# Weight loads traced as far as raw tiles are free, an eighth raw tile, and 128-row bias products in the expert stage

## The chip, the cores and the metric

One core of one Trainium2 chip runs the whole program in one launch. The metric is the device time of that launch in microseconds (us); the time before is the median of three runs. The engines are TensorE (PE, its weight loads are PEld), VectorE (DVE), ScalarE (ACT), GpSimd (POOL) and SyncE (SP, which issues nearly all DMAs).

## What is computed

The reference is a chain of two blocks over 512 tokens of width 1024, all in float32. The part that the change touches is the mixture of experts at the end of the first block:

```python
logits = h @ w_router + b_router              # 512 tokens, 32 experts
top_val, top_idx = lax.top_k(logits, 4)
gates = softmax(top_val)
# for each expert e, on the rows xb that chose it:
u   = xb @ w1[e] + b1[e]                       # 1024 -> 2048
glu = minimum(u[:, 0::2], 7.0); lin = clip(u[:, 1::2], -7.0, 7.0)
act = glu * sigmoid(1.702 * glu) * (lin + 1.0)
y   = act @ w2[e] + b2[e]                      # 1024 -> 1024
# out[token] += gate * y
```

Before it stand a token mixer (recurrence, Fourier mixing) with its output projection; behind it two layers of attention (three branches), gates and projections.

## The kernel before, in words

The 32 experts are sorted by how many tokens chose them; a rank has a fixed number of rows (`CAP`, L1246): 192 for ranks 0 to 5, 128 for ranks 6 to 14, 64 for the rest. Ranks run in groups (`sequence`, L1259). Six groups have four ranks A, B, C, D: A has 192 rows, C has 128, B and D have 64. Two groups have three ranks (64, 128, 64 rows) and one has two (64, 128). The order inside a group is written out by hand (`order`, L1276): four column blocks of w1 (0 to 3) and two of w2 (4, 5) for each rank. In most four-rank groups A and B alternate first, then C and D alternate, then the w2 blocks follow.

A block of 512 columns is worked off in four parts of 256 weight rows. Each part is one raw tile of 128 x 2 x 512 floats, 512 KB. `Weights` (L1296) streams them: `load` (L1305) has SP issue the DMA into a tile of the pool `wraw` (seven tiles), `split` (L1316) makes a high and a low half of it (`whi` by ACT on L1324, `wlo` by DVE on L1328 and POOL on L1329) in a pool of four, and `next` (L1352) hands the oldest part to the matmuls. Ranks of 128 rows (`whole`, L1254) take the raw tile itself (L1702), so it is free only when their matmuls are done. Ranks of 64 or 192 rows take the two halves (L1706, L1707, L1709), so the raw tile is free when it is split. `ahead` (L1338) says how far loads and splits are traced ahead of use: before, loads up to seven parts, splits up to three. After that a scheduler orders each engine's instructions; each engine runs its own list in order and waits on semaphores where a tile is not ready or not yet free. SP's list in this stage is the 768 weight loads and a few others.

In `up` (L1822) the first matmul of each accumulation is the bias (L1833): its stationary side is a selection of this rank's row of `b1`, 64 rows (32 of the high half, 32 of the low). For 64-row blocks POOL copies that selection into `mhalf` first (L1827). `consts2` (L1417) loads and splits `b1`; `route` (L1489) makes `perm`. `swiglu` (L1711) runs behind each w1 block: ACT `us`, DVE `gl` and `ln`, ACT `sg`, POOL `ln` (L1728), and then PE transposes `ln` (L1687) for w2. `overflow` (L2007) stands ahead of the expert loop and is a branch that is not taken with these inputs (no instruction inside it is in the trace).

The second block has its own `Weights` with three raw tiles and the same class (L3084).

Of the kernel before, what the change touches and what calls it, by code (L numbers as in the profile page):

```python
# [8 lines left out]
F = mybir.dt.float32  # L9
R = mybir.dt.float32r  # L10
# [1285 lines left out]
class Weights:  # L1296


    def __init__(self, tc, ctx, raw=7, parts=4, kn=2, side="left"):
        self.tc, self.nc, self.kn = tc, tc.nc, kn  # L1300
        self.nraw, self.nsplit = raw, parts - 1
        self.raw = ctx.enter_context(tc.tile_pool(name="wraw", bufs=raw, side=side, reuse_waits="tile"))
        self.par = ctx.enter_context(tc.tile_pool(name="wpar", bufs=parts, side=side, reuse_waits="tile"))
# [31 lines left out]

    reach = 4

    def ahead(self, loads, splits):  # L1338
        while len(self.loads) < min(self.used + loads, len(self.parts)):
            m, k0 = self.parts[len(self.loads)][:2]  # L1340
            self.loads.append(self.load(m(), k0))
        isplit = lambda j: self.parts[j][-1] is not False
        n = sum(isplit(j) for j in range(self.used, len(self.splits)))
        while len(self.splits) < min(len(self.loads), self.used + self.reach):
            j = len(self.splits)
            if isplit(j):
                if n >= splits:
                    break
                n += 1
            self.splits.append(self.split(self.loads[j]) if isplit(j) else self.loads[j][0])  # L1350

    def next(self, splits=None):  # L1352
        self.ahead(self.nraw, self.nsplit if splits is None else splits)
        out = self.splits[self.used]
        self.used += 1
        return out


def consts_moe():
# [10 lines left out]
    lim = np.array([[float(max(128 * j, CAP[r])) if 128 * (j + 1) > CAP[r] else 1e6 for r in range(32) for j in range(4)]], np.float32)  # L1370
    two = np.concatenate([iota[:, :64], iota[:, :64]], 1)
    return {"m_cap": caps, "m_tri": tri, "m_tie": tie, "m_first": first, "m_iota": iota, "m_two": two, "m_tok": tok, "m_lim": lim}


class Moe:
# [13 lines left out]
    def consts(self):  # L1389
# [8 lines left out]
        nc.sync.dma_start(self.iota, rowbc(I["m_iota"], 512))  # L1398
        self.two = c.tile([128, 128], F, name="mtwo")
        nc.sync.dma_start(self.two, rowbc(I["m_two"], 128))  # L1400
        self.tokf = c.tile([128, 5], F, name="mtokf")
# [9 lines left out]
        nc.sync.dma_start(self.br, rowbc(I["b_router"][0:1, :], 32))  # L1411
        self.cap = c.tile([128, 32], F, name="mcap")
        nc.sync.dma_start(self.cap, rowbc(I["m_cap"], 32))
        self.wr = c.tile([128, 8, 32], F, name="mwr")
        nc.sync.dma_start(self.wr, I["w_router"][0].rearrange("(k p) e -> p k e", p=128))

    def consts2(self, pool):  # L1417

        nc, I, c = self.nc, self.i, self.c
        self.halves = [c.tile([64, 128], R, name=f"mhalf{a}") for a in range(2)]  # L1420
        self.b1 = c.tile([64, 2048], R, name="mb1")
        zero = pool.tile([64, 128], F, name="mz", tag="mz", bufs=1)
        nc.gpsimd.memset(zero, 0.0)
        for t in self.halves:
            nc.gpsimd.tensor_copy(t, zero)
        for a in range(2):
            t = pool.tile([128, 1024], F, name="mb1r", tag="fxh", bufs=2)
            s = slice(a * 1024, (a + 1) * 1024)
            t = t[0:32]
            nc.sync.dma_start(t, I["b1"][0][:, s])  # L1430
            nc.scalar.activation(self.b1[0:32, s], t, AF.Copy)
            nc.gpsimd.tensor_tensor(self.b1[32:64, s], t, self.b1[0:32, s].bitcast(F), op=OP.subtract)

# [55 lines left out]
    def route(self):  # L1489
# [37 lines left out]
        nc.vector.tensor_scalar(perm, self.iota[:32, :E], rank, None, op0=OP.is_equal)  # L1527
        self.perm = c.tile([64, E], R, name="permr")
        nc.vector.tensor_copy(self.perm[0:32], perm)
        nc.vector.tensor_copy(self.perm[32:64], perm)  # L1530
        dr = tt.tile([32, E], F, name="drank")
# [100 lines left out]
    def hots(self, r0, n, start, two, posm=None):  # L1632

        nc = self.nc
        iob = (self.two if two else self.iota)[:, None, :128].to_broadcast([128, n, 128])
        hot = []
        for t in range(4):
            h = self.g.tile([128, 4, 128], BF, name="hot", tag="hot", bufs=4)
            src = (self.posm if posm is None else posm)[:, t, r0:r0 + n]
            if start:  # L1640
                s2 = self.g.tile([128, 8], F, name="hots", tag="hots", bufs=4)
                nc.vector.tensor_scalar(s2[:, :n], src, -float(start), None, op0=OP.add)
                src = s2[:, :n]
            nc.vector.tensor_tensor(h[:, :n], iob, src[:, :, None].to_broadcast([128, n, 128]), op=OP.is_equal)
            hot.append(h)
# [65 lines left out]
    def swiglu(self, ps, act, c, tag=None):  # L1711
# [8 lines left out]
        v = ps.rearrange("p (n a) -> p n a", a=2)  # L1720
        gl = x_.tile([128, 256], F, name="gl", tag="gl", bufs=2)
        ln = x_.tile([128, 256], F, name="ln", tag="ln", bufs=3)
        sg = x_.tile([128, 256], F, name="sg", tag="sgm", bufs=2)
        nc.vector.tensor_scalar(gl[:m], v[:, :, 0], 7.0, None, op0=OP.min)  # L1724
# [31 lines left out]
    def plan(self, before):  # L1756
# [23 lines left out]

        first = [(lambda m=m: [m], k0) for m, k0 in before]
        self.W.stream(first + sum([parts(r, a, cc) for g in sequence() for a, r, cc in order(g)], []))

    def experts(self, hD, x1, gt2):
# [37 lines left out]
        def up(r, cc):  # L1822
# [3 lines left out]
            if cc == 0 and not whole(r):  # L1826
                nc.gpsimd.tensor_copy(half[:, 0:64], self.perm[:, r:r + 1].bitcast(F).to_broadcast([64, 64]))  # L1827
            for k0 in range(0, 8, kn):
                w = self.W.next()
                for p, xx in zip(ps, x):  # L1830
                    if k0 == 0:
                        pm = half if xx.n == 64 else self.perm[:, r:r + 1].to_broadcast([64, 128])
                        nc.tensor.matmul(p, pm, self.b1[:, cc * 512:(cc + 1) * 512], start=True, stop=False)  # L1833
                    self.mm_part(p, xx, w, k0, False, k0 + kn == 8)
# [114 lines left out]
        for t in range(4):  # L1949
            for a in range(2):  # L1950
                nc.scalar.activation(self.acc[t][:, a * 512:(a + 1) * 512], self.iota, AF.Copy, scale=0.0)
        self.overflow(hD)
        gs = groups()
        where = {r: min(sum(not whole(q) for q in g[:j]), 1) for g in seq for j, r in enumerate(g)}
# [52 lines left out]
    def overflow(self, hD):  # L2007
# [9 lines left out]
        with tc.If(ne > 0):  # L2017
# [19 lines left out]
            with tc.For_i(0, 128, 1) as i:  # L2037
                te = x_.tile([1, 2], I32, name="te", tag="te", bufs=1)
                nc.sync.dma_start(te, tD[bass.ds(i, 1), :])
                on = nc.values_load(te[0:1, 0:1], min_val=0, max_val=1)  # L2040
                with tc.If(on > 0):
                    e = nc.values_load(te[0:1, 1:2], engines=[ET.SP], min_val=0, max_val=31)
                    ix = x_.tile([128, 1], I32, name="ix", tag="ix", bufs=1)
                    nc.sync.dma_start(ix, iD[bass.ds(i, 1), :].rearrange("a p -> p a"))
# [25 lines left out]
            nc.vector.tensor_tensor(row, self.later[3], offs[:, None, :].to_broadcast([128, 4, 32]), op=OP.add)  # L2070

            over = c.tile([128, 4, 32], F, name="over")
            nc.vector.tensor_tensor(over, self.later[3], self.cap[:, None, :].to_broadcast([128, 4, 32]), op=OP.is_ge)
            gto = self.pick(over, "gto", x_, "y")
# [1034 lines left out]
```

## Time and profile before

| what | value |
|---|---|
| three runs | 3784.77, 3789.82, 3796.57 us (median 3789.82) |
| the profiled execution | 3795.27 us |
| its span, first to last instruction | 3793.5 us, TensorE clock granted 0.924 on average |
| busy share of the span | PE 90%, PEld 66%, DVE 66%, ACT 45%, POOL 46% |
| weight loads of the experts | 768, first issued at 706.0 us, last at 2375.1 us |
| second block, 2500 to 3700 us | PE busy 1176.8 of 1200 us, clock 1.00, DMA share 0.26 |

Matmuls are pipelined, and the profile models their ends: a busy PE is not a PE at its peak. What a matmul costs in a full stream is the distance from its start to the next start. The DMA share is the mean busy share of the core's 16 DMA engines.

### The profile page before, as it was taken

Reading aid. Unit: us, or ns where it says so; the run is one execution under the profiler, and the core shown is the slowest. Engines: PE = TensorE matmul, PEld = TensorE weight load, DVE = VectorE, ACT = ScalarE, POOL = GpSimd, SP = SyncE. Lnnn points to the kernel's source line nnn. Section 1 sums busy time; section 2 is a strip of 40 time slices with the busy share of each in tenths; the row PEclk is TensorE's granted clock in tenths of the full one; section 3 lists DMA queues with packets and bytes.
Section 4 is the critical chain, followed back from the end, with each engine's and each line's share of the span. In section 5 each row is a group of like instructions: output and inputs, shape, how many; then the busy total and the mean of one; then the engine's idle time right before and its main releaser. Section 6 shows DMA issues by size and latency. Waiting matters only on the chain. (4 is left out here: it accounts for less than half of the span.)

```text
span 3793.5 us, 51274 instructions
## 1 busy us (share of the span) xinstructions
PE 3424.3 (90%) x16864; PEld 2510.5 (66%) x16864; DVE 2510.3 (66%) x4793; ACT 1696.9 (45%) x2937; POOL 1734.7 (46%) x1509
## 2 busy tenths in 40 slices
PE   7966679769898999999899989799999999999999
PEld 4756567645565565656465655488878878887887
DVE  7778875667786787766786856754566445546653
ACT  4634323224555555545555544444434434343442
POOL 4444333435665666555675755433342342334223
PEclk9976677869899999999999989899999999999999
DMA  7853243627778888877878788532221243223113
GB/s 255 265 141 83 65 104 92 211 98 249 248 234 276 290 285 279 263 263 262 295 258 294 239 273 290 174 90 75 74 85 51 61 140 101 79 73 84 40 51 106
DMA packets 420649, 653.86 MB, mean 172 GB/s; under 512 B 83939, under 2 KB 145568, under 8 KB 419862
## 3 DMA queue, kind: packets, MB, share of 16 engines
q1 hardware_dynamic: 414650, 633.32, 52.2%
q0 software_dynamic: 4000, 13.90, 1.2%
q10 hardware_dynamic: 1724, 3.28, 0.3%
q8 instruction: 135, 2.21, 0.2%
q14 instruction: 140, 1.15, 0.1%
HBM read 610.80 MB, written 39.61 MB: 171 GB/s over the span
## 5 line engine op out<-in xcount | busy, mean ns | idle before, releaser
L1329 POOL TENSOR_TENSOR wlo<-wraw,whi 128x288 fp32r<-128x288 f32 x736 | 957.3, 1311 | 1001.7 <-ACT whi L1324 935.2
L1328 DVE TENSOR_TENSOR wlo<-wraw,whi 128x736 fp32r<-128x736 f32 x736 | 828.5, 1133 | 472.4 <-ACT whi L1324 458.5
L1324 ACT ACTIVATE whi<-wraw 128x1024 fp32r<-128x1024 f32 x736 | 769.9, 1056 | 609.8 <-DMA wraw<-in_w 193.3
L2275 PE MATMUL psg<-whi,xh 128*128 128x512 f32 (+1 forms) x1152 | 472.4, 410 | 0.3 <-ACT xh L2292 0.3
L2277 PE MATMUL psg<-whi,xl 128*128 128x512 f32 (+1 forms) x1152 | 451.2, 392 | 0.0
L2276 PE MATMUL psg<-wlo,xh 128*128 128x512 f32 (+1 forms) x1152 | 449.7, 391 | 0.0
L1707 PE MATMUL ps<-wlo,x 128*128 128x512 f32 x928 | 383.7, 413 | 29.9 <-DVE wlo L1328 25.6
L1706 PE MATMUL ps<-whi,x 128*128 128x512 f32 x928 | 393.6, 424 | 1.0 <-ACT whi L1324 0.8
L1702 PE MATMUL ps<-wraw,x 128*128 128x512 f32 x576 | 277.4, 634 | 0.0
L2277 PEld LDWEIGHTS psg<-whi,xl 128*128 128x128 f32 x1152 | 217.5, 189 | 42.3
L1728 POOL TENSOR_TENSOR ln<-ln,sg 64x256 f32<-64x256 f32 (+1 forms) x152 | 166.5, 1096 | 163.9 <-DVE ln L1727 107.7
L2275 PEld LDWEIGHTS psg<-whi,xh 128*128 128x128 f32 x1152 | 218.1, 189 | 35.0 <-ACT xh L2292 1.5
L2276 PEld LDWEIGHTS psg<-wlo,xh 128*128 128x128 f32 x1152 | 218.3, 189 | 34.5
L1707 PEld LDWEIGHTS ps<-wlo,x 128*128 128x128 f32 x928 | 179.4, 193 | 91.9 <-DVE wlo L1328 44.7
L1706 PEld LDWEIGHTS ps<-whi,x 128*128 128x128 f32 x928 | 179.5, 193 | 72.1 <-issue 23.3
L1707 PE MATMUL ps<-wlo,a 128*128 128x512 f32 x464 | 195.8, 422 | 8.9 <-DVE wlo L1328 4.8
L1702 PEld LDWEIGHTS ps<-wraw,x 128*128 128x128 f32 x576 | 111.9, 201 | 136.2 <-issue 135.3
L1706 PE MATMUL ps<-whi,a 128*128 128x512 f32 x464 | 195.1, 421 | 1.5 <-ACT whi L1324 1.4
L2415 ACT ACTIVATE pexp<-pss,mx 128x128 f32<-128x128 f32 x192 | 101.0, 527 | 154.7 <-DVE mx L2410 66.6
L1726 ACT ACTIVATE sg<-gl 64x256 f32<-64x256 f32 (+1 forms) x152 | 62.9, 414 | 168.6 <-DVE gl L1724 153.6
L1702 PE MATMUL ps<-wraw,a 128*128 128x512 f32 x288 | 138.3, 619 | 0.0
L1707 PEld LDWEIGHTS ps<-wlo,a 128*128 128x128 f32 x464 | 90.6, 195 | 47.8 <-DVE wlo L1328 16.4
(736 smaller groups left out, 6927.8 us busy)
## 6 DMA issues: line engine op xcount, KB each, us to landing
wraw<-in_w SPq DMA_DIRECT2D x768, 512.0 KB
wraw<-in_w_in SPq DMA_DIRECT2D x140, 512.0 KB
mraw<-in_w_ada SPq DMA_DIRECT2D x32, 512.0 KB
wraw<-in_w_out SPq DMA_DIRECT2D x24, 512.0 KB
wada<-in_w_ada SPq DMA_DIRECT2D x16, 512.0 KB
wraw<-in_w_mem_kv SPq DMA_DIRECT2D x16, 512.0 KB
wraw<-in_w_branch_m SPq DMA_DIRECT2D x8, 512.0 KB
wraw<-in_w_branch_b SPq DMA_DIRECT2D x8, 512.0 KB
```

The costliest lines, as they stand in the source:

```text
L1324: nc.scalar.activation(hi, raw, AF.Copy)
L1328: nc.vector.tensor_tensor(lw[:, :m], rw[:, :m], hw[:, :m].bitcast(F), op=OP.subtract)
L1329: nc.gpsimd.tensor_tensor(lw[:, m:], rw[:, m:], hw[:, m:].bitcast(F), op=OP.subtract)
L1702: nc.tensor.matmul(ps, a, w[:, k], start=s, stop=e)
L1706: nc.tensor.matmul(ps, a, hi[:, k], start=s, stop=False)
L1707: nc.tensor.matmul(ps, a, lo[:, k], start=False, stop=e and not two)
L1726: nc.scalar.activation(sg[:m], gl[:m], AF.Sigmoid, scale=1.702)
L1728: nc.gpsimd.tensor_tensor(ln[:m], ln[:m], sg[:m], op=OP.mult)
L2275: nc.tensor.matmul(p, xh[:, kk], hi[:, k, :n], start=kk == 0, stop=False)
L2276: nc.tensor.matmul(p, xh[:, kk], lo[:, k, :n], start=False, stop=False)
L2277: nc.tensor.matmul(p, xl[:, kk], hi[:, k, :n], start=False, stop=kk == kch - 1)
L2415: nc.scalar.activation(p[:, :n], s[:, :n], AF.Exp, bias=nm, scale=-1.0, accum_out=H["d"][:, i:i + 1])
```

## The change

- `Weights` has eight raw tiles where it had seven. `ahead` now traces loads as far as the tile that a load would take has had its last reader traced (its split, or, for a 128-row rank, its matmuls): `fetch`. Until the expert loop begins the old rule holds (`free = False`) with a limit of 15 parts in all.
- The biases `b1` take 128 rows of 1024 columns: high and low half of the first 1024 columns, then of the second. `perm` and `halves` get a second version, zero where the other half stands, and the bias product runs over 128 rows. POOL makes two copies (128 x 64) for each 64- or 192-row rank where it made one (64 x 64).
- Room is made: the constant `two` goes (its comparison reads `iota` in two pieces), `cap` is loaded inside the untaken branch, `gl` and `sg` share three buffers where they had two each, two small tiles swap tags.

```diff
-    def __init__(self, tc, ctx, raw=7, parts=4, kn=2, side="left"):
+    def __init__(self, tc, ctx, raw=8, parts=4, kn=2, side="left"):
...
-    reach = 4
+    reach, free = 4, True
+    limit = None
     def ahead(self, loads, splits):
-        while len(self.loads) < min(self.used + loads, len(self.parts)):
-            m, k0 = self.parts[len(self.loads)][:2]
-            self.loads.append(self.load(m(), k0))
         isplit = lambda j: self.parts[j][-1] is not False
+        def fetch():
+            top = min(len(self.parts), self.limit or len(self.parts))
+            while len(self.loads) < top:
+                j = len(self.loads)
+                q = j - self.nraw
+                if j >= self.used + loads if loads else q >= 0 and q >= (len(self.splits) if isplit(q) else self.used):
+                    break
+                m, k0 = self.parts[j][:2]
+                self.loads.append(self.load(m(), k0))
+        fetch()
...
             self.splits.append(self.split(self.loads[j]) if isplit(j) else self.loads[j][0])
+        fetch()
     def next(self, splits=None):
-        self.ahead(self.nraw, self.nsplit if splits is None else splits)
+        self.ahead(0 if self.free else self.nraw, self.nsplit if splits is None else splits)
...
-        self.halves = [c.tile([64, 128], R, name=f"mhalf{a}") for a in range(2)]
-        self.b1 = c.tile([64, 2048], R, name="mb1")
+        self.halves = [[c.tile([128, 128], R, name=f"mhalf{a}{b}") for b in range(2)] for a in range(2)]
+        self.b1 = c.tile([128, 1024], R, name="mb1")
...
-        self.two = c.tile([128, 128], F, name="mtwo")
-        nc.sync.dma_start(self.two, rowbc(I["m_two"], 128))
...
-            nc.vector.tensor_tensor(h[:, :n], iob, src[:, :, None].to_broadcast([128, n, 128]), op=OP.is_equal)
+            nc.vector.tensor_tensor(h[:, :n].rearrange("p n (a j) -> p n a j", a=a), iob, src[:, :, None, None].to_broadcast([128, n, a, 128 // a]), op=OP.is_equal)
...
+            cap = x_.tile([128, 32], F, name="mcap", tag="te", bufs=1)
+            nc.sync.dma_start(cap, rowbc(I["m_cap"], 32))
...
-        self.perm = c.tile([64, E], R, name="permr")
-        nc.vector.tensor_copy(self.perm[0:32], perm)
-        nc.vector.tensor_copy(self.perm[32:64], perm)
+        for a in range(4):
+            nc.vector.tensor_copy(self.perm[a * 32:a * 32 + 32, a // 2], perm)
...
-        gl = x_.tile([128, 256], F, name="gl", tag="gl", bufs=2)
+        gl = x_.tile([128, 256], F, name="gl", tag="gl", bufs=3)
-        sg = x_.tile([128, 256], F, name="sg", tag="sgm", bufs=2)
+        sg = x_.tile([128, 256], F, name="sg", tag="gl", bufs=3)
...
+        self.W.free, self.W.limit = False, len(first) + 7
...
             if cc == 0 and not whole(r):
-                nc.gpsimd.tensor_copy(half[:, 0:64], self.perm[:, r:r + 1].bitcast(F).to_broadcast([64, 64]))
+                for a in range(2):
+                    nc.gpsimd.tensor_copy(half[a][:, 0:64], self.perm[:, a, r:r + 1].bitcast(F).to_broadcast([128, 64]))
...
-                        pm = half if xx.n == 64 else self.perm[:, r:r + 1].to_broadcast([64, 128])
-                        nc.tensor.matmul(p, pm, self.b1[:, cc * 512:(cc + 1) * 512], start=True, stop=False)
+                        pm = half[cc // 2] if xx.n == 64 else self.perm[:, cc // 2, r:r + 1].to_broadcast([128, 128])
+                        nc.tensor.matmul(p, pm, self.b1[:, cc % 2 * 512:(cc % 2 + 1) * 512], start=True, stop=False)
...
         self.overflow(hD)
+        self.W.limit, self.W.free = None, True
```

The instruction lists of the five engines keep their work but not their places. Two places matter here.

SP, in the fourth group (ranks 2, 19, 8, 20), where the w1 blocks of rank 8 (128 rows) and rank 20 (64 rows) alternate: the loads of block 1 of rank 20 (four parts) and the first two of the block after it. A register row (`ISA`) ahead of each load is left out. PE behind "waits" means that the tile's last user was a matmul of a 128-row rank; DVE and Pool mean that it was a split. Before:

```order
L1312 DMA wraw<-in_w 128x2x512 [waits DMAHW6_49,DVE_49,Pool_49]
L1312 DMA wraw<-in_w 128x2x512 [waits PE_49]
L1312 DMA wraw<-in_w 128x2x512 [waits PE_49]
L1312 DMA wraw<-in_w 128x2x512 [waits DMAHW3_49,DVE_49,Pool_49]
L1312 DMA wraw<-in_w 128x2x512 [waits DMAHW7_49,PE_49]
L1312 DMA wraw<-in_w 128x2x512 [waits DMAHW0_49,DMAHW4_49,DVE_49,Pool_49]
```

The same six loads in the changed kernel:

```order
L1312 DMA wraw<-in_w 128x2x512 [waits PE_49]
L1312 DMA wraw<-in_w 128x2x512 [waits DMAHW1_49,DVE_49,Pool_49]
L1312 DMA wraw<-in_w 128x2x512 [waits PE_49]
L1312 DMA wraw<-in_w 128x2x512 [waits PE_49]
L1312 DMA wraw<-in_w 128x2x512 [waits DMAHW2_49,DMAHW6_49,DVE_49,Pool_49]
L1312 DMA wraw<-in_w 128x2x512 [waits DMAHW3_49,DMAHW7_49,DVE_49,Pool_49]
```

Before, the fourth of them takes the tile of the first (three loads earlier, so it waits for that part's own split); in the changed kernel it takes a tile that rank 8's block 0 has used, and the first tile to be taken again within four loads is the next one's.

ACT, at the same place: the splits from the last of the A and B blocks into the first of the C and D blocks, and the swiglu steps between them. Before:

```order
L1324 ACTIVATE whi<-wraw 128x1024 x4
L1726 ACTIVATE sg<-gl 128x256
L1324 ACTIVATE whi<-wraw 128x1024 x3
L1717 ACTIVATE us<-ps 64x512
L1324 ACTIVATE whi<-wraw 128x1024 x2
L1726 ACTIVATE sg<-gl 64x256
L1717 ACTIVATE us<-ps 64x512
L1324 ACTIVATE whi<-wraw 128x1024
L1690 ACTIVATE a<-ps 128x256
```

In the changed kernel (L1727 is the former L1717, L1736 the former L1726, L1700 the former L1690):

```order
L1324 ACTIVATE whi<-wraw 128x1024 x2
L1736 ACTIVATE sg<-gl 128x256
L1324 ACTIVATE whi<-wraw 128x1024 x4
L1727 ACTIVATE us<-ps 64x512
L1324 ACTIVATE whi<-wraw 128x1024 x3
L1736 ACTIVATE sg<-gl 64x256
L1700 ACTIVATE a<-ps 128x256
L1324 ACTIVATE whi<-wraw 128x1024
L1727 ACTIVATE us<-ps 64x512
```

One to two splits more stand ahead of the same `us` and `sg`.

## Rows read from the trace of the kernel before

**Rows 1.** Busy time by stretch, sum of 13 stretches without 192-row ranks; three of them
```profile
core 0: us, PE busy (x) PEld busy (x) DVE busy (x) ACT busy (x) POOL busy (x), PEclk, DMA share, GB/s
1447.00:1505.00 58.00, 55.83 (x162) 28.66 (x161) 36.54 (x57) 27.02 (x43) 29.51 (x28) 0.91 0.85 274
1505.00:1570.00 65.00, 61.02 (x234) 40.54 (x235) 49.73 (x56) 40.08 (x51) 39.15 (x31) 0.97 0.92 311
...
1649.00:1715.00 66.00, 54.33 (x166) 29.08 (x165) 38.16 (x61) 28.82 (x46) 33.29 (x31) 0.90 0.83 283
...
sum 846.00, PE 758.85 PEld 431.47 DVE 584.16 ACT 420.68 POOL 491.05; mean PE 58.37 PEld 33.19 DVE 44.94 ACT 32.36 POOL 37.77
```

**Rows 2.** The same view: sum of the eight stretches between; two of them
```profile
1379.00:1447.00 68.00, 67.16 (x280) 48.82 (x280) 63.04 (x85) 42.57 (x59) 52.12 (x43) 1.00 0.79 256
...
1715.00:1774.00 59.00, 58.76 (x224) 41.09 (x224) 37.69 (x44) 35.83 (x43) 34.14 (x24) 0.97 0.82 282
...
sum 533.00, PE 528.48 PEld 375.02 DVE 424.88 ACT 319.96 POOL 360.82; mean PE 66.06 PEld 46.88 DVE 53.11 ACT 39.99 POOL 45.10
```

**Rows 3.** The same view: 14 us in which several loads were under way at once
```profile
1500.00:1514.00 14.00, 13.44 (x59) 10.27 (x58) 13.32 (x17) 9.81 (x14) 9.97 (x10) 1.00 1.00 361
```

**Rows 4.** Waits of SP's own queue, 900 to 2376 us: total, times, longest
```profile
SPq L1312 <- DVE wlo L1328: 652.8, 461, 9.8
SPq L1312 <- POOL wlo L1329: 232.6, 337, 4.6
SPq L1312 <- PE ps L1702: 133.4, 71, 8.9
```

**Rows 5.** Waits of all engines, 900 to 2376 us
```profile
ACT whi L1324 <- DMA wraw<-in_w: 191.1, 146, 7.8
...
PE ps L1687 <- POOL ln L1728: 51.7, 17, 6.8
...
PE ps L1707 <- DVE wlo L1328: 29.9, 38, 3.5
```

**Rows 6.** SP's waits in the fourth group, 1459 to 1470 us
```profile
SPq L1312 <- DVE wlo L1328: 9.4, 1, 9.4
```

**Rows 7.** ACT in order of time, fourth group: start, length, what, [idle before <-releaser]
```profile
1458.69 0.26 ACT L1690 ACTIVATE a<-ps 128x128 fp32r<-128x128 f32 x1
1466.14 1.06 ACT L1324 ACTIVATE whi<-wraw 128x1024 fp32r<-128x1024 f32 x1 [7.19 <-DMA wraw<-in_w]
...
1472.89 1.06 ACT L1324 ACTIVATE whi<-wraw 128x1024 fp32r<-128x1024 f32 x1 [1.08 <-DMA wraw<-in_w]
```

**Rows 8.** PE in order of time, the same place
```profile
1460.24 0.47 PE L1833 MATMUL ps<-mb,permr 64*128 64x512 f32 x1
1460.64 7.13 PE L1702 MATMUL ps<-wraw,x 128*128 128x512 f32 x16
1467.61 0.38 PE L1687 MATMUL ps<-ident,ln 128*128 128x128 f32 x2
1467.92 0.50 PE L1833 MATMUL ps<-mb,mhalf 64*128 64x512 f32 x1
1468.35 0.51 PE L1706 MATMUL ps<-whi,x 128*128 128x512 f32 x1
...
1469.24 0.40 PE L1706 MATMUL ps<-whi,x 128*128 128x512 f32 x1
1469.48 0.39 PE L1707 MATMUL ps<-wlo,x 128*128 128x512 f32 x1
...
1473.45 0.80 PE L1707 MATMUL ps<-wlo,x 128*128 128x512 f32 x1 [1.51 <-DVE wlo L1328]
```

**Rows 9.** PE's groups by form in the stretch 1649 to 1715 us: count, busy, mean
```profile
L1702 PE MATMUL ps<-wraw,x 128*128 128x512 f32 x64 | 29.1, 602 | 0.0
L1706 PE MATMUL ps<-whi,x 128*128 128x512 f32 x32 | 14.6, 456 | 0.0
L1707 PE MATMUL ps<-wlo,x 128*128 128x512 f32 x32 | 14.1, 442 | 0.6 <-POOL wlo L1329 0.5
```

**Rows 10.** The bias matmuls and POOL's copies for them, by source line: shortest/median/longest ns
```profile
L1833 PE MATMUL ps<-mb,mhalf x92: 469/492/792, 819.6 to 2343.3; 64*128 64x512 f32 x92
L1833 PE MATMUL ps<-mb,permr x60: 469/490/792, 816.1 to 2355.5; 64*128 64x512 f32 x60
...
L1827 POOL CAST mhalf<-permr x23: 226/295/941, 799.5 to 2166.2; 64x64 fp32r<-64x64 f32 x23
```

More of the change, by code (lines that the diff above doesn't have):

```diff
@@ L1370, in consts_moe @@
     lim = np.array([[float(max(128 * j, CAP[r])) if 128 * (j + 1) > CAP[r] else 1e6 for r in range(32) for j in range(4)]], np.float32)
-    two = np.concatenate([iota[:, :64], iota[:, :64]], 1)
-    return {"m_cap": caps, "m_tri": tri, "m_tie": tie, "m_first": first, "m_iota": iota, "m_two": two, "m_tok": tok, "m_lim": lim}
+    return {"m_cap": caps, "m_tri": tri, "m_tie": tie, "m_first": first, "m_iota": iota, "m_tok": tok, "m_lim": lim}
 class Moe:
@@ L1411, in consts @@
         nc.sync.dma_start(self.br, rowbc(I["b_router"][0:1, :], 32))
-        self.cap = c.tile([128, 32], F, name="mcap")
-        nc.sync.dma_start(self.cap, rowbc(I["m_cap"], 32))
         self.wr = c.tile([128, 8, 32], F, name="mwr")
@@ L1419, in consts2 @@
         nc, I, c = self.nc, self.i, self.c
-        self.halves = [c.tile([64, 128], R, name=f"mhalf{a}") for a in range(2)]
-        self.b1 = c.tile([64, 2048], R, name="mb1")
-        zero = pool.tile([64, 128], F, name="mz", tag="mz", bufs=1)
+        self.halves = [[c.tile([128, 128], R, name=f"mhalf{a}{b}") for b in range(2)] for a in range(2)]
+        self.b1 = c.tile([128, 1024], R, name="mb1")
+        zero = pool.tile([128, 1024], F, name="mb1r", tag="fxh", bufs=2)[:, :128]
         nc.gpsimd.memset(zero, 0.0)
-        for t in self.halves:
+        self.perm = c.tile([128, 2, 32], R, name="permr")
+        nc.gpsimd.tensor_copy(self.perm.rearrange("p c e -> p (c e)"), zero[:, :64])
+        for t in self.halves[0] + self.halves[1]:
             nc.gpsimd.tensor_copy(t, zero)
@@ L1428, in consts2 @@
             s = slice(a * 1024, (a + 1) * 1024)
[L1429 to L1432, printed above, removed]
+            p = slice(a * 64, a * 64 + 32)
+            nc.sync.dma_start(t[p], I["b1"][0][:, s])
+            nc.scalar.activation(self.b1[p], t[p], AF.Copy)
+            nc.gpsimd.tensor_tensor(self.b1[a * 64 + 32:a * 64 + 64], t[p], self.b1[p].bitcast(F), op=OP.subtract)
     def logits(self, t, hT):
@@ L1634, in hots @@
         nc = self.nc
-        iob = (self.two if two else self.iota)[:, None, :128].to_broadcast([128, n, 128])
+        a = 2 if two else 1
+        iob = self.iota[:, None, None, :128 // a].to_broadcast([128, n, a, 128 // a])
         hot = []
@@ L2037, in overflow @@
             with tc.For_i(0, 128, 1) as i:
-                te = x_.tile([1, 2], I32, name="te", tag="te", bufs=1)
+                te = x_.tile([1, 2], I32, name="te", tag="ix", bufs=1)
                 nc.sync.dma_start(te, tD[bass.ds(i, 1), :])
@@ L2042, in overflow @@
                     e = nc.values_load(te[0:1, 1:2], engines=[ET.SP], min_val=0, max_val=31)
-                    ix = x_.tile([128, 1], I32, name="ix", tag="ix", bufs=1)
+                    ix = x_.tile([128, 1], I32, name="ix", tag="te", bufs=1)
                     nc.sync.dma_start(ix, iD[bass.ds(i, 1), :].rearrange("a p -> p a"))
@@ L2070, in overflow @@
             nc.vector.tensor_tensor(row, self.later[3], offs[:, None, :].to_broadcast([128, 4, 32]), op=OP.add)
+            cap = x_.tile([128, 32], F, name="mcap", tag="te", bufs=1)
+            nc.sync.dma_start(cap, rowbc(I["m_cap"], 32))
             over = c.tile([128, 4, 32], F, name="over")
-            nc.vector.tensor_tensor(over, self.later[3], self.cap[:, None, :].to_broadcast([128, 4, 32]), op=OP.is_ge)
+            nc.vector.tensor_tensor(over, self.later[3], cap[:, None, :].to_broadcast([128, 4, 32]), op=OP.is_ge)
             gto = self.pick(over, "gto", x_, "y")
```

## The prediction

> **What bounds the kernel now.** I first read the page's sums: PE is busy 90% of the span, so a second look is needed at where it is not, and at what kind of busy that is. Cut by stretches, the expert stage (about 817 to 2376 us) falls into two kinds. In eight stretches with a 192-row rank, 533 us in all, PE is busy 528.48 us [rows 2]: matmuls set the time there, and a weight that comes earlier buys nothing. In thirteen others, 846 us in all, blocks of 64- and 128-row ranks alternate, or w2 blocks follow. Each 512 KB part feeds few matmuls there; PE shows 758.85 us busy, PEld only 431.47, and the DMA share is 0.83 to 0.92 in the three shown [rows 1]. That "busy" is stretched. In the stretch from 1649 to 1715 us the 64 matmuls of L1702 have a mean of 602 ns, and sixteen of them in a stream take 6.97 us from their first start to the next instruction's (1460.64 to 1467.61), 0.436 each [rows 8, 9]. A stream of L1706 and L1707 goes at 0.24 (1469.24 to 1469.48) [rows 8]. So the matmuls of that stretch need 64 x 0.436 + 64 x 0.24 = 43 us, and with the bias products and transposes about 49 of its 66. The remainder is starvation.
>
> What starves PE? The thirteen stretches hold 432 parts (six alternations of C and D with 32 each, two three-rank groups with 72 each, two w2 runs and the two-rank group with 32 each). 846 / 432 = 1.96 us per 524,288 bytes, or 268 GB/s. Where several loads were under way at once the same queue moved 361 GB/s at a share of 1.00 [rows 3], which is 1.45 us per part. The transfers can go faster, then, if more of them are under way. SP's own queue says why they are not: from 900 to 2376 us it stands 652.8 + 232.6 + 133.4 = 1018.8 of 1476 us waiting for a raw tile's reader [rows 4]. SP sends a load at once when its tile is free. The ring of seven tiles is the limit, and ACT in its turn waits 191.1 us, 146 times, for a tile to land [rows 5].
>
> One place shows the chain. SP waits 9.4 us for a split [rows 6]: the fourth load of rank 20's block was given the tile of the first, so it cannot leave before that part has landed and been split. ACT has nothing to split for 7.19 us and starts at 1466.14 [rows 7]; PE then waits 1.51 us for the low half at 1473.45 [rows 8].
>
> **The change, part by part.**
>
> *Tracing further ahead.* Alone it sends nothing earlier: SP runs its list in order and waits on semaphores, not on the program's order. What it can change is which tile a load takes. In the place above the fourth load now takes a tile that rank 8's block 0 has given up, so the 9.4 us wait [rows 6] has no cause there; the first tile taken again within four loads is the next one's. I price this together with the eighth tile.
>
> *The eighth tile.* Seven tiles at 1.96 us each mean that a tile comes round every 13.7 us. If a round stayed that long, eight tiles would give 1.71 us per part and 740 us in place of 846: -106. But a round includes time in the transfer queue, and that grows as the queue fills. Bounds: nothing (a), if each new load waits for the same late reader; -127 (b), if the transfer engines were never idle, since a share of 0.85 of 1.96 us is 1.67 us of their time per part and 432 x 1.67 = 719 [rows 1]; and at the very end -219, with all parts at the 1.45 us of [rows 3]. The nearest row is the best stretch that the same alternation reached with seven tiles, a share of 0.92 where its neighbours have 0.85 and 0.83 [rows 1]: 846 x (1 - 0.85/0.92) = 64. I take **-64**. In the eight stretches where PE is full [rows 2] the tile is worth nothing. What is late next once ACT has its tiles: the low half, for which PE already waits 29.9 us, and POOL's `ln` with 51.7 us [rows 5].
>
> *128-row bias products.* The 92 + 60 bias matmuls [rows 10] use 64 rows. From the start of one to the start of its successor it is 0.43 us (1467.92 to 1468.35) and 0.40 us (1460.24 to 1460.64); a 128-row matmul of 512 columns in a stream has 0.24 [rows 8]. If the bias product becomes like its neighbours, each gives back 0.16 to 0.19, together some 27 us. The 64-row product stands alone among 128-row ones, so its extra may be the switch or something else that stays; the lower bound is therefore 0, the upper 27. About a third of them lie where PE waits for weights anyway and hide there. I take **-18**.
>
> The Trainium skill (TensorE: Matmul & The Clock Gate, section LDWEIGHTS) has a rule against this term: the time of a weight load goes by its columns, and one of 32 contraction rows takes as long as one of 128. By that rule 64 and 128 rows would cost the same and this term would be 0. The trace does not agree as far as starts go: 0.43 against 0.24 [rows 8], whether that comes from the load or from a switch of shape.
>
> *POOL's copies.* 23 blocks get a second copy of `mhalf`, at a median of 295 ns and at most 941 [rows 10]: 7 to 22 us on POOL, with the rows doubled but the columns the same. POOL is busy 491.05 of 846 us [rows 1], and the copy is made at a rank's first block, ahead of `wlo` pieces. Mostly hidden; at worst all 22 us. With the few added casts in `route` and `consts2` I take **+2**.
>
> *At no cost:* the tables `hots` compares have the same size as before; the load of `cap` moves into the branch not taken, and with `two` gone SP issues two small loads fewer. `gl` and `sg` share three buffers, so a `gl` now waits for POOL's `ln` two blocks earlier, which PE has as a rule already used. If that cover went, the price would appear as PE waiting for `ln`, now 51.7 us [rows 5]. On SP nothing else is passed by: its list here is the loads. The last loads go out a little earlier, and those behind them with them. Block 2 keeps three raw tiles.
>
> **Sum.** 3795.3 (the profiled execution) - 64 - 18 + 2 = 3715. That execution lies 5.5 us above the median of the three runs, so against the median: **3710 us**.
>
> **Rivals.**
>
> 1. *The ring gives nothing.* The tile is free earlier, but the parts come no faster, because what gates them is the reader at the far end (for the 128-row ranks a matmul on PE, 133.4 us of SP's wait) or the transfers themselves. For it: shares of 0.83 to 0.92 are high already [rows 1]. Against: 361 GB/s at a share of 1.00 in [rows 3]. Then only the bias term is left: 3790 - 18 = 3772, or 3790 if that fails too.
>
> 2. *Slower: ACT's list.* The added look-ahead puts one or two more splits ahead of `us` and `sg`. ACT runs in order. If the tile of such a split has not landed when ACT comes to it, `us` waits with it, `ln` is late, and PE stands at the transposes as it already does 17 times [rows 5]. The row nearest to such a wait is 7.19 us [rows 7]; one at each of the six places where C and D begin is 43 us. With the ring giving nothing and the bias 18: 3790 - 18 + 43 = 3815. It decides when the added split's tile lands later than `us` could run; the eighth tile pushes the other way, since the tile lands earlier.
>
> 3. *Full lifting.* The transfers keep the rate of [rows 3], 627 us for the 432 parts: 3790 - 219 - 18 = 3553. About 49 of 66 us of PE work would nearly allow it. Against: at every change from one kind of block to another the ring must refill, and one tile is 1/7 more, not a third.
>
> 4. *The change does not do what it says.* The pool may hand out tiles in an order that undoes the eighth (a load given a tile that is free late, as in [rows 6]), and the bias gap remains: 3790, no change.
>
> **How the numbers follow.** Forecast (ring partly lifted, bias mostly) 0.74; rival 1 0.11; rival 2 0.06; rival 3 0.04; rival 4 0.05. The range goes from 3790 - 127 - 18, rounded down to 3640, up to rival 1 at 3772; rivals 2, 3 and 4 and a part of 1 lie outside. A measurement of this kernel can tell about 0.3%, 11 us. Faster by more than that: forecast, rival 3 and most of rival 1, 0.87; within it: rival 4 and the rest of rival 1, 0.07; slower: rival 2, 0.06.
>
> **What would show it.** SP's waits in 900 to 2376 us fall, and not one by one into the same sum under another reader; ACT's 191.1 us for landings falls to about 100; the thirteen stretches get shorter by some 5 us each with a share of 0.90 or more, while the eight stay within 1 or 2 us apart from their bias products; the 7.19 us at rank 20 is gone; a bias product starts 0.24 us ahead of its successor. Wrong, if the shares stay as they are with the tile there (rival 1), if PE's wait for `ln` grows well beyond 51.7 us with ACT behind an unlanded tile (rival 2), if the bias products still take 0.4 us, or if time is gained or lost outside 817 to 2376 us.

## The result and the profile after

The changed kernel takes 3742.89 us (median of four runs; the kernel before 3787.59 beside it): a ratio of 0.9873 with an interval of 0.9854 to 0.9893, 1.3% or 45 us faster. One of the four runs took 3898.54 us at a mean granted clock of 0.807 and is left out of the ratio. A second series gave 0.9886 (0.9866 to 0.9905). The forecast was 80 us, so the direction and the range held, and a little over half of the gain came.

The thirteen stretches of [rows 1], cut again at the first matmul of the same blocks (same columns, changed kernel):

```profile
1434.00:1490.00 56.00, 51.67 (x164) 29.30 (x163) 34.33 (x58) 26.70 (x43) 35.05 (x31) 0.94 0.89 293
1490.00:1553.00 63.00, 59.35 (x234) 40.93 (x233) 47.10 (x54) 37.51 (x49) 35.03 (x29) 0.97 0.92 307
1629.00:1693.00 64.00, 52.60 (x166) 30.07 (x165) 36.97 (x62) 28.45 (x46) 37.94 (x32) 0.90 0.88 296
...
sum 810.00, PE 717.13 PEld 432.61 DVE 572.98 ACT 415.39 POOL 508.79; mean PE 55.16 PEld 33.28 DVE 44.08 ACT 31.95 POOL 39.14
```

They went from 846 to 810 us, 2.8 each. The third answers to 1649 to 1715 in [rows 1]: 66 us became 64, the share went from 0.83 to 0.88, and PE is still busy for only 52.60 of 64. The eight stretches of [rows 2] went from 533 to 524 us, about what the 61 bias products in them give back at 0.16 us each (an estimate, 10 us). The waits of all engines from 900 us to the end of the stage, in the changed kernel (total, times, longest):

```profile
ACT whi L1324 <- DMA wraw<-in_w: 129.5, 87, 5.8
...
PE ps L1697 <- POOL ln L1738: 62.0, 20, 5.6
...
PE ps L1717 <- DVE wlo L1328: 22.7, 14, 3.2
```

Against [rows 5], ACT waits a third less for landings (191.1 to 129.5). But PE's wait for `ln`, the largest that PE has, did not fall: 51.7 us before, 62.0 now. SP's own queue over the same time, in the changed kernel:

```profile
SPq L1312 <- DVE wlo L1328: 593.1, 439, 8.1
SPq L1312 <- POOL wlo L1329: 266.7, 364, 3.2
SPq L1312 <- PE ps L1712: 100.5, 59, 7.3
```

Together 960 of 1431 us, or 67%, where [rows 4] had 69%. With one tile more SP waits for a free tile nearly as much as before, so this share does not tell how much time the ring costs.

The place of [rows 7] and [rows 8], ACT in order of time, changed kernel:

```profile
1443.78 0.28 ACT L1700 ACTIVATE a<-ps 128x128 fp32r<-128x128 f32 x1 [0.65 <-PE ps L1697]
1448.04 1.06 ACT L1324 ACTIVATE whi<-wraw 128x1024 fp32r<-128x1024 f32 x1 [3.99 <-DMA wraw<-in_w]
1449.42 1.06 ACT L1324 ACTIVATE whi<-wraw 128x1024 fp32r<-128x1024 f32 x1 [0.32 <-DMA wraw<-in_w]
```

The wait of 7.19 us is 3.99 us: shorter, not gone. And the place where the rest of the time went, PE at the end of the C and D blocks of the fifth group (the stretch 1629 to 1693):

```profile
1677.90 0.47 PE L1697 MATMUL ps<-ident,ln 64*128 64x64 f32 x2 [4.76 <-POOL ln L1738]
1680.33 0.69 PE L1697 MATMUL ps<-ident,ln 128*128 128x128 f32 x2 [1.96 <-POOL ln L1738]
1680.67 0.78 PE L1845 MATMUL ps<-mb,mhalf 128*128 128x512 f32 x1
1681.24 0.63 PE L1716 MATMUL ps<-whi,x 128*128 128x512 f32 x1
1681.67 0.63 PE L1717 MATMUL ps<-wlo,x 128*128 128x512 f32 x1
...
1686.88 0.39 PE L1716 MATMUL ps<-whi,x 128*128 128x512 f32 x1
1687.10 0.40 PE L1717 MATMUL ps<-wlo,x 128*128 128x512 f32 x1
1692.15 0.47 PE L1697 MATMUL ps<-ident,ln 64*128 64x64 f32 x2 [4.65 <-POOL ln L1738]
```

Three waits, 11.4 us of the stretch's 64, and in none of them does PE itself wait for a weight. A late weight has a part in the first, by way of ACT and DVE. In their lists the steps from `gl` to that `ln` stand behind the splits of a tile for which ACT waited 4.71 us and, after it, DVE 5.00:

```profile
1671.01 1.06 ACT L1324 ACTIVATE whi<-wraw 128x1024 fp32r<-128x1024 f32 x1 [4.71 <-DMA wraw<-in_w]
1673.33 0.40 ACT L1736 ACTIVATE sg<-gl 64x256 f32<-64x256 f32 x1
...
1666.83 0.27 DVE L1734 TENSOR_SCALAR gl<-us 64x256 f32<-64x256 f32 x1
1672.10 0.93 DVE L1328 TENSOR_TENSOR wlo<-wraw,whi 128x736 fp32r<-128x736 f32 x1 [5.00 <-ACT whi L1324]
1674.59 1.00 DVE L1737 SCALAR_TENSOR_TENSOR ln<-ln,gl 64x256 f32<-64x256 f32 x1
```

Behind the first two waits the matmuls go at 0.43 us from start to start (1681.24 to 1681.67) and only later at 0.22 (1686.88 to 1687.10). The same stretch by short pieces (columns as in [rows 1]):

```profile
1660.00:1672.00 12.00, 11.98 (x40) 6.69 (x39) 6.10 (x11) 4.10 (x7) 5.17 (x5) 1.00 0.99 344
1672.00:1678.00 6.00, 1.24 (x6) 0.47 (x5) 5.87 (x9) 4.09 (x7) 5.43 (x4) 0.85 0.67 202
1681.00:1686.00 5.00, 5.00 (x14) 3.84 (x13) 1.32 (x2) 2.50 (x3) 2.13 (x3) 0.50 0.97 306
```

PE had been full at a granted clock of 1.00, stood for `ln` with 1.24 us busy of six, and then ran at 0.50, the lower of the two levels (1.2 of 2.4 GHz). So a wait costs more than its length: 5 us at half the clock are some 2.5 us of work lost (an estimate), on top of the 6.7 us of the two waits.

### The profile page after: what moved, and what is told of

Read it like the earlier page. It is cut to its first block, busy times and chain, and to the rows that moved or that the text cites. A ratio compares the mean times of both kernels' runs of the same rounds, so it can differ in the third digit from the quotient of the medians.

```text
span 3739.6 us, 51475 instructions
## 1 busy us (share of the span) xinstructions
PE 3357.5 (90%) x16864; PEld 2518.3 (67%) x16864; DVE 2501.3 (67%) x4795; ACT 1691.4 (45%) x2937; POOL 1761.2 (47%) x1535
## 5 line engine op out<-in xcount | busy, mean ns | idle before, releaser
L1329 POOL TENSOR_TENSOR wlo<-wraw,whi 128x288 fp32r<-128x288 f32 x736 | 976.9, 1338 | 934.7 <-ACT whi L1324 871.1
L1328 DVE TENSOR_TENSOR wlo<-wraw,whi 128x736 fp32r<-128x736 f32 x736 | 814.5, 1115 | 426.2 <-ACT whi L1324 411.5
L1717 PE MATMUL ps<-wlo,x 128*128 128x512 f32 x928 | 381.1, 411 | 32.2 <-DVE wlo L1328 21.8
L1716 PE MATMUL ps<-whi,x 128*128 128x512 f32 x928 | 381.3, 411 | 0.1
L1712 PE MATMUL ps<-wraw,x 128*128 128x512 f32 x576 | 265.9, 613 | 0.0
L1717 PEld LDWEIGHTS ps<-wlo,x 128*128 128x128 f32 x928 | 180.5, 195 | 91.7 <-DVE wlo L1328 32.4
L1717 PE MATMUL ps<-wlo,a 128*128 128x512 f32 x464 | 190.8, 411 | 5.8 <-POOL wlo L1329 4.4
L1736 ACT ACTIVATE sg<-gl 64x256 f32<-64x256 f32 (+1 forms) x152 | 63.0, 414 | 160.2 <-DVE gl L1734 152.4
L1697 PE MATMUL ps<-ident,ln 64*128 64x64 f32 (+1 forms) x304 | 57.1, 272 | 67.5 <-POOL ln L1738 67.5
```

The source lines that it names most:

```text
L1328: nc.vector.tensor_tensor(lw[:, :m], rw[:, :m], hw[:, :m].bitcast(F), op=OP.subtract)
L1329: nc.gpsimd.tensor_tensor(lw[:, m:], rw[:, m:], hw[:, m:].bitcast(F), op=OP.subtract)
L1712: nc.tensor.matmul(ps, a, w[:, k], start=s, stop=e)
L1716: nc.tensor.matmul(ps, a, hi[:, k], start=s, stop=False)
L1717: nc.tensor.matmul(ps, a, lo[:, k], start=False, stop=e and not two)
L1736: nc.scalar.activation(sg[:m], gl[:m], AF.Sigmoid, scale=1.702)
```

## The experiments

Each was timed in five rounds beside the kernel before on the same chip. Theory A: the ring is the larger part of the gain and the bias the smaller. Theory B: the bias is nearly all. Theory C: the order in which tiles are taken matters.

**1. The bias alone.** The kernel before with the new `consts2`, `perm` and the copies and products of `up`; seven tiles, old rule.

```diff
-        self.b1 = c.tile([64, 2048], R, name="mb1")
+        self.b1 = c.tile([128, 1024], R, name="mb1")
...
-                        pm = half if xx.n == 64 else self.perm[:, r:r + 1].to_broadcast([64, 128])
+                        pm = half[cc // 2] if xx.n == 64 else self.perm[:, cc // 2, r:r + 1].to_broadcast([128, 128])
```

> The kernel before with the 128-row bias products alone (seven tiles, old tracing rule). In the trace of the changed kernel the 152 bias products take 49.3 us from their start to the next start where they took 68.2, and the gap ahead of them 28.7 where it was 35.1: 25 us less on PE. Theory A (the ring is the larger part, the bias the smaller): most of the 25 us reach the end, 12 to 25 us faster, about 3768 us. Theory B (the bias product is nearly all of the 45 us): 3743 to 3752 us. Theory C (the order in which tiles are taken is the larger part): as A, 3768 us.

Measured: 3762.02 us, ratio 0.9948 (0.9926 to 0.9970): 20 us, between 11 and 28. Theory B falls.

**2. Seven tiles in the changed kernel.**

```diff
-    def __init__(self, tc, ctx, raw=8, parts=4, kn=2, side="left"):
+    def __init__(self, tc, ctx, raw=7, parts=4, kn=2, side="left"):
```

> The changed kernel with seven raw tiles: new tracing rule and 128-row biases, no eighth tile. Theory A (eighth tile): the rule alone gives nothing, so as the bias alone, about 3768 us, and SP's wait sums of 900 to 2376 us near those of before. Theory B (bias): about as the changed kernel, 3743 to 3750 us. Theory C (the rule, by the order in which tiles are taken): 3743 to 3755 us too, but with the bias alone at 3768.

Measured: 3771.03 us, ratio 0.9965 (0.9950 to 0.9979). The rule brought nothing at seven tiles: the intervals of this run and the one before overlap, so the 6 us between them are not told from none. ACT's wait for landings is as long as in [rows 5], from 900 us to the end of the stage:

```profile
ACT whi L1324 <- DMA wraw<-in_w: 193.5, 128, 7.6
```

**3. Eight tiles with the old rule.** Loads traced as many parts ahead as there are tiles, throughout.

```diff
-    reach, free = 4, True
+    reach, free = 4, False
...
-        self.W.limit, self.W.free = None, True
+        self.W.limit = None
```

> The changed kernel with the old tracing rule throughout (loads traced as many parts ahead as there are tiles), eight tiles, 128-row biases. Theory A (eighth tile): as the changed kernel, 3743 us within 6. Theory B (bias): the same. Theory C (the rule): 3755 to 3770 us, with waits of SP for a split three or four loads earlier still there.

Measured: 3746.95 us, ratio 0.9896 (0.9866 to 0.9925), which overlaps with the changed kernel's. Theory C falls: the new tracing rule does not decide, the tile does. The traces show why. The order of splits and `sg` on ACT is in run 2 that of the kernel before and in run 3 that of the changed kernel, and ACT's wait at rank 20 (7.19 us before, 3.99 after) is 7.31 us in run 2 and 3.69 in run 3. So both places that the section on the change shows come from the eighth tile, and the new rule left them as they were. By the ratios of the runs with seven tiles (0.9965) and eight (0.9896, 0.9886, 0.9873) the tile is worth 26 to 35 us; by the two runs with the old rule (run 1 and this one) it is 20.

**4. Six tiles.** As run 2, with `raw=6`.

> The changed kernel with six raw tiles. Theory A (the ring is the limit): every tile counts more the fewer there are; going from seven to six costs more than the eighth gives, 35 to 90 us above the run with seven tiles, so about 3810 to 3850 us. Theory B or C (the ring is not the limit): within 15 us of the run with seven tiles.

Measured: 3826.29 us, ratio 1.0120 (1.0092 to 1.0148), so the step from seven to six costs 0.0155, some 59 us. Theory A holds: the ring is a limit, and the eighth tile gives less than the seventh. That left a question: with 846 us of stretches in which PE was far from its matmuls' need, why did the tile give only some 30 us? Theory D: much of that time is PE's wait for `ln`. Theory E: the ring or the transfers set the pace, and PE would only wait for weights instead.

**5. No wait for `ln`.** The transposes read a constant, so the second product does not get the swiglu's result.

```diff
-        self.todo.append((self.now + LATE, tag, lambda: self.transposed(ln, 2, act, 2 * c)))
+        self.todo.append((self.now + LATE, tag, lambda: self.transposed(self.iota, 2, act, 2 * c)))
```

> The changed kernel, but the transposes behind the swiglu read a constant tile in place of ln, so PE no longer waits for POOL there (the rest of the swiglu is still computed; the second product then works on constants). In the changed kernel PE stands 67.5 us, 22 times, for ln (62.0 of it in 900 to 2376 us). Theory D (what I took for starvation by the ring is in good part this wait, which no raw tile shortens): the changed kernel less 45 to 70 us, about 3675 to 3700 us. Theory E (the ring or the transfers set the pace, and PE would only wait for weights instead): 3725 us or more.

Measured: 3679.27 us, ratio 0.9722 (0.9701 to 0.9744): against the changed kernel's 0.9873, 57 us, and the matmuls, loads and splits are the same in number. Theory D holds.

**6. The same with seven tiles.**

> The same with seven raw tiles. With PE's wait for ln gone the ring is what is left: theory D expects the eighth tile to be worth more than the 24 us that it gave (run with seven tiles against the changed kernel), 30 to 60 us. Theory E expects the same 24 us or less.

Measured: 3716.53 us, ratio 0.9814 (0.9797 to 0.9831). The eighth tile is worth 35 us here by the ratios, at the upper end of the 26 to 35 above; alone this tells the two apart weakly.

**7. Splits traced three parts ahead.** `reach` 3 in place of 4.

> The changed kernel with splits traced three parts ahead of use in place of four, so one split fewer stands ahead of us and sg in ACT's list. If late splits ahead of sg cause PE's waits for ln (at 1671.01 ACT waits 4.71 us for a landing with sg behind it, and PE then 4.76 us): 10 to 25 us faster than the changed kernel. If the splits come too late instead, PE's wait for the low half (22.7 us in 900 to 2376) grows and the time is the same or up to 30 us longer.

Measured: 3739.37 us, ratio 0.9872 (0.9855 to 0.9889), the changed kernel's own. PE waits for `ln` 59.9 us from 900 us on (62.0 without the edit). But the edit did not do what it was meant to: in its trace each of the 152 `sg` has as many splits ahead of it in ACT's list as in the changed kernel (of the 138 `us` of 64-row blocks three have one fewer). So whether splits ahead of `sg` make PE wait was not tested.

**8. Transposes put off six parts in place of four.**

```diff
-        self.todo.append((self.now + LATE, tag, lambda: self.transposed(ln, 2, act, 2 * c)))
+        self.todo.append((self.now + LATE + 2, tag, lambda: self.transposed(ln, 2, act, 2 * c)))
```

> The changed kernel with the transposes of ln put off six parts in place of four, so that two more parts of matmuls stand ahead of them on PE. Theory D: the wait for ln falls from 67.5 us to 20 or less, and 30 to 50 us are gained, about 3695 to 3715 us. Theory E: 3735 to 3745 us, with the wait for ln gone but waits for weights in its place.

Measured: 3726.03 us, ratio 0.9839 (0.9823 to 0.9856): some 13 us gained, but PE's wait for `ln` hardly fell, to 63.6 us (67.5 counted in the same way for the changed kernel). So a number of parts by which transposes are put off is not what places the costly ones. What fell is PE's wait for the part of the low half that DVE makes, 22.7 to 9.7 us; why was not tried.

The code then showed what does place them. In `experts` a gather of new rows (L1954) first calls `need(q)` for the rank whose row buffer it takes. `need` works off everything that is pending for that rank. The transposes of `x`, which read that buffer, carry the rank as their tag, and so do the rank's swiglu and the transposes of `ln`. At the end of C and D this pulls a swiglu up to right behind the block that made its input, and its transposes right behind that.

**9 to 11. The changed kernel again, a tag of its own for `x`, and both edits.** Run 10 has this edit alone (and the same tag in the two calls of `need` ahead of a product with `x`); in run 11 `need` also takes only the asked transposes out of the queue, and those of `ln` are put off six parts.

```diff
-                    self.todo.append((self.now, r, lambda x=x, p=p, k0=k0: self.transposed(x[:, k0 * 128:(k0 + 4) * 128], 4, p, k0)))
+                    self.todo.append((self.now, ("x", r), lambda x=x, p=p, k0=k0: self.transposed(x[:, k0 * 128:(k0 + 4) * 128], 4, p, k0)))
...
-                at[min(get, unp[r])].insert(0, lambda r=r, q=oldr: (self.need(q[-1]) if q else None, fetch(r)))
+                at[min(get, unp[r])].insert(0, lambda r=r, q=oldr: (self.need(("x", q[-1])) if q else None, fetch(r)))
```

> The changed kernel itself once more, beside the next two on one chip: about 3743 us, and within 0.3% of its first measurement.

> The changed kernel with a tag of their own for the transposes of x. Before a gather reuses its buffer, need() asks for one rank's pending work; the tag is the rank, so it also traces that rank's swiglu and the transposes of ln at once, right behind the block that made them, and PE stands until POOL has made ln (three waits of 4.8, 2.0 and 4.7 us between 1677 and 1693). With the own tag only the transposes of x are asked for. Theory D (these waits are what the tiles cannot shorten): the wait for ln falls from 67.5 us to 30 or less, 20 to 40 us faster than the changed kernel, about 3703 to 3723 us. Theory E: 3735 us or more.

> The same, with need() taking only the asked transposes out of their queue, and the transposes of ln put off six parts in place of four. Theory D: at best what the kernel without the wait for ln showed (3679 us), as a rule between that and the run above, 3680 to 3710 us.

Measured: 3739.22 us (0.9886, 0.9866 to 0.9905), 3687.06 us (0.9757, 0.9732 to 0.9781) and 3668.49 us (0.9700, 0.9679 to 0.9720). The tag alone gains 49 us on the changed kernel by the ratios, more than expected. The waits of PE from 900 us to the end of the stage in run 10:

```profile
PE ps L1717 <- DVE wlo L1328: 26.4, 26, 2.7
PE ps L1717 <- POOL wlo L1329: 17.8, 22, 2.3
PE ps L1697 <- DMA xg<-hD,idxi: 10.1, 5, 3.6
PE ps L1697 <- POOL ln L1738: 9.7, 5, 3.9
```

The wait for `ln` is 9.7 us where it was 62.0; those for the low half grew from 36.6 to 44.2 in sum. The same C and D blocks as above, by stretch, in run 10:

```profile
1595.00:1645.00 50.00, 48.80 (x162) 27.06 (x160) 31.42 (x53) 23.85 (x39) 31.31 (x27) 1.00 0.89 305
```

and in run 11:

```profile
1590.00:1640.00 50.00, 49.51 (x168) 28.11 (x167) 34.11 (x54) 26.84 (x42) 32.56 (x29) 1.00 0.96 334
```

The blocks that took 66 us before and 64 after the change take 50, close to the 49 that the prediction had put together for their matmuls, and the granted clock is 1.00 where it was 0.90. ACT still waits 108.2 us for landings in run 10, but PE no longer stands for the `ln` that comes late by it. Run 11 is the fastest kernel here: 3.0% under the kernel before and 1.9% under the changed one by the ratios.

**12. Run 11 with seven tiles.**

> The kernel of the run before (own tag for x, transposes later) with seven raw tiles. Between seven and eight tiles the changed kernel shows 24 to 32 us, and without the wait for ln 37. If the wait for ln hides part of what a tile is worth: 35 to 50 us slower than with eight, about 3703 to 3719 us. If a tile's worth does not depend on it: 24 to 32 us, 3692 to 3700 us.

Measured: 3716.18 us, ratio 0.9831 (0.9811 to 0.9851). Against 0.9700 the eighth tile is worth 50 us here, some 39 to 60 by the two intervals (an estimate), where it was worth 26 to 35 in the changed kernel. That is what was expected if the wait for `ln` hides part of what the tile is worth. It is not shown: in runs 5 and 6 that wait is gone as well and the tile is worth 35 us, and run 11 differs from the changed kernel by three edits at once.

## Why the prediction was right in direction and too large

**The ring.** That SP's wait for a free tile limits the prefetch was right: runs 2, 3 and 4 show 59 us from six to seven tiles and some 30 from seven to eight. The term was -64 and came to -20 to -35. The step that failed is "The remainder is starvation": the 17 us of the stretch from 1649 to 1715 that matmuls did not need were all given to late weights, and the gain was then drawn from the whole 846 us by the DMA share. In that stretch before the change PE stood 11.1 us for `ln` in two waits and 0.5 us for a weight, and from 1700 to 1705 us the granted clock was 0.50:

```profile
PE ps L1687 <- POOL ln L1728: 11.1, 2, 6.3
PE ps L1707 <- POOL wlo L1329: 0.5, 2, 0.3
```

[rows 5] held the sum, 51.7 us, and the prediction named it as what would be late next, not as what was already there. Runs 5 and 10 show it: without that wait 57 and 49 us come, with the tiles unchanged. Late weights have a part in it by way of ACT and DVE, as the place above shows; how large a part stays open. But more tiles do not shorten it: it is 58.4 us with six tiles (run 4), 51.7 to 53.5 with seven (before, runs 1 and 2) and 58.3 to 63.9 with eight (the changed kernel, runs 3 and 9), from 900 us to the end of the stage.

PE's own waits for the halves of a weight are small over the whole stage. Before the change they were 29.9 us for DVE's part [rows 5], 7.0 for POOL's and 2.3 for ACT's half, 39.2 us in all and less than the 64 that were to be gained. In run 2 and in the changed kernel, which differ by the tile alone, they are 55.1 and 36.9 us:

```profile
PE ps L1717 <- DVE wlo L1328: 38.5, 50, 3.3
PE ps L1717 <- POOL wlo L1329: 13.1, 19, 1.4
PE ps L1716 <- ACT whi L1324: 3.5, 7, 1.2
...
PE ps L1717 <- DVE wlo L1328: 22.7, 14, 3.2
PE ps L1717 <- POOL wlo L1329: 13.9, 19, 2.6
PE ps L1716 <- ACT whi L1324: 0.3, 2, 0.2
```

The size of the term was also read from a wrong row. The stretch with a share of 0.92 (1505 to 1570 us) is not the same alternation: most of its matmuls read the swiglu's result `a` (64 of L1707, 63 of L1706, 32 of L1702), so it is a run of w2 blocks. The six alternations of C and D had shares of 0.83 to 0.85.

In two of the six places where C and D alternate the wait for `ln` was absent before. In the fourth group (1447 to 1505 us) and the seventh (1976 to 2034) PE waited for the low half instead, 1.9 and 3.1 us, and in the fourth the clock behind the longest of these waits was 0.56 (1472 to 1480 us). There the reading fits. Yet 58 us became 56 in the one and 54 in the other, where the four other places shrank by 2, 2, 2 and 7.

**Tracing further ahead.** "Alone it sends nothing earlier" held (run 2 against run 1, run 3 against the changed kernel). That the rule changes which tile a load takes did not: the better choice at rank 20, 7.19 to 3.99 us, came with the eighth tile (7.31 us in run 2, 3.69 in run 3).

**The bias.** The term of -18 measured 20 us in run 1. That the values agree is in part luck. At the upper clock level all products had 0.40 to 0.43 us to the next start before. Now one in a stream has 0.24, and one behind a transpose 0.32; PE in order of time, changed kernel:

```profile
834.25 0.40 PE L1717 MATMUL ps<-wlo,x 128*128 128x512 f32 x1
834.48 0.40 PE L1845 MATMUL ps<-mb,permr 128*128 128x512 f32 x1
834.72 0.39 PE L1716 MATMUL ps<-whi,x 128*128 128x512 f32 x1
...
1649.00 0.38 PE L1697 MATMUL ps<-ident,ln 128*128 128x128 f32 x2
1649.13 0.48 PE L1845 MATMUL ps<-mb,mhalf 128*128 128x512 f32 x1
1649.45 0.39 PE L1716 MATMUL ps<-whi,x 128*128 128x512 f32 x1
```

The 0.32 us are no loss. From the first of the two transposes to the start behind that product 0.45 us pass (1649.00 to 1649.45), and two transposes of 128 rows in a stream (0.11 each) and one such matmul (0.23) take as long; the second transpose has only 0.03 to the next start.

The sum was larger than forecast. Over the 152 products the traces of the kernel before and of run 1 differ by 17.6 us from a product's start to the next one, by 7.4 from the start ahead of it and by 16.4 from its successor's start to the one behind, 41 us together; the prediction counted the first part alone. About half of the 41 us reached the end, where it had expected two thirds of 27.

The weight load itself did not change with the rows. The loads of the bias products before, with 64 rows, by source line (shortest/median/longest ns):

```profile
L1833 PEld LDWEIGHTS ps<-mb,mhalf x92: 182/183/333, 819.6 to 2343.2; 64*128 64x128 f32 x92
```

and after, with 128:

```profile
L1845 PEld LDWEIGHTS ps<-mb,mhalf x92: 186/188/338, 825.0 to 2297.0; 128*128 128x128 f32 x92
```

183 and 188 ns at the median, so the rule of the Trainium skill (TensorE: Matmul & The Clock Gate, section LDWEIGHTS) that the load goes by columns agrees with the trace. It says nothing on the time between two matmuls, and that is where the 20 us lay. The Trainium skill (TensorEngine Tiling (Array Packing), section Key Properties) has a rule that fits that part: a change of the tiling mode drains the engine. The 64-row product among 128-row ones was such a change, and its extra 0.19 us went with it. The trace agrees at another place too, where the product itself has no part: a transpose of 64 rows among 128-row matmuls, in the kernel before.

```profile
1658.39 0.39 PE L1706 MATMUL ps<-whi,x 128*128 128x512 f32 x1
1658.62 0.40 PE L1707 MATMUL ps<-wlo,x 128*128 128x512 f32 x1
1658.95 0.34 PE L1687 MATMUL ps<-ident,ln 64*128 64x64 f32 x2
1659.21 0.50 PE L1706 MATMUL ps<-whi,x 128*128 128x512 f32 x1
1659.55 0.40 PE L1707 MATMUL ps<-wlo,x 128*128 128x512 f32 x1
```

The matmul ahead of it has 0.33 us to the next start and the one behind it 0.34, where 0.23 is usual. Ahead of a transpose of 128 rows it stays 0.23 (median of 45 at the upper clock level). The 128-row neighbours of a 64-row bias product had the same 0.33 and 0.34 before. No run separates the switch from the row count for the product's own 0.19 us.

**POOL's copies**, +2, lie inside run 1 and were not measured apart. The copy over 128 rows has a median of 237 ns (46 of them), less than the one over 64 [rows 10]. POOL's wait for PE ahead of these copies rose from 5.4 to 15.9 us.

**The signals.** ACT's wait for landings fell to 129.5 us where about 100 was expected. The stretches shrank by 2.8 us each, not 5, with a share of 0.82 to 0.96, and 0.90 or more in six of the thirteen. SP's waits, which were to fall, kept their share of the time (69 to 67%), and the wait at rank 20 was shorter, not gone. The range held because it reached to the case with the ring giving nothing.

**The rivals.** Rival 1 had the right warning, that the parts might not come faster, with the wrong cause. Rival 2 saw the right wait: PE does stand at the transposes for `ln`, in the kernel before already. Its chain is in the trace of the changed kernel as well. At five places ACT waits 3.2 to 4.7 us for a landing shortly ahead of an `sg`, and PE then 2.5 to 4.8 us for the `ln`, 18.7 of the 67.5 us. With eight tiles 50 of the 152 `sg` have one to four splits more ahead of them than with seven, and PE's wait for `ln` is 5 to 12 us longer. Whether these splits cause that was not tested, since run 7 left the order of splits and `sg` as it was. What run 10 shows is that the order in which `need` puts the transposes decides whether PE stands. Rivals 3 and 4 did not happen.

## What to carry to other kernels

Before an engine's idle time is put down to late data, split it by what ended each wait, stretch by stretch, and subtract the waits that the change does not touch: 11.1 us of one stretch's 17 were a transpose that waited for an elementwise product. Then follow that product back: here a part of the wait began with a late weight on two other engines. More buffers gave less with each one: 59 us for the seventh tile, some 30 for the eighth. What the eighth is worth beside other edits came out at 35 to 50 us, and why it differs is open. Where a helper flushes "everything of this item" before a buffer is reused, see what else it pulls forward: a tag of its own for the work that was meant gained about as much as the whole change (49 against 45 us). After an edit that should move work in a list, see in the trace that it moved: run 7 came out equal because it had not.

## What the runs showed that was not expected

A wait of PE costs more than its length. After 4.76 and 1.96 us of standing for `ln` the granted clock was 0.50 for the next 5 us, with matmuls 0.43 us apart, while the stretch without those waits (run 10) ran at 1.00. From 900 us to the end of the stage the mean granted clock was 0.96 in the changed kernel and 0.98 in run 10. A row count that differs from its neighbours' costs those neighbours too: some 0.1 us to the next start on the 128-row matmul ahead of a 64-row instruction, and as much on the one behind it.
